# DRAM scratch in blocks of 512 elements, and the prompt's values read back from the output

## The chip, the core and the metric

The kernel runs on one core of a Trainium2 chip. A core has five engines with a queue of instructions each: TensorE (PE in the profile, with its weight loads as PEld), VectorE (DVE), ScalarE (ACT), GpSimd (POOL) and SyncE (SP). DMAs are issued from SyncE's queue nearly always, some from ScalarE's, and run on 16 DMA engines. The metric is device time in microseconds, lower is better.

## What is computed

One step of a decoder with two layers over a prompt of 2048 tokens and over 8 samples of 8 new tokens each, whose past of 4096 tokens lies in a paged cache. All data are 32-bit floats.

```python
# layer A: a gated linear recurrence; layer B: attention with forget gates
x = x + rms_norm(recurrent_mixer(rms_norm(x, a_pre_norm), ...), a_post_norm)
z = rms_norm(x, kv_norm) @ w_kv                  # the shared K, V and forget logits
k, v, logf = z[..., :1024], z[..., 1024:2048], log_sigmoid(z[..., 2048:] + b_f)
c = cumsum(logf)                                 # over the past and the new tokens
q, g = split(rms_norm(x, b_pre_norm) @ b_w_in)
s = q @ k.T * 64 ** -0.5 + c[query] - c[key]     # 16 heads of 64, causal
o = softmax(s) @ v
x = x + rms_norm((o * silu(g)) @ b_w_out, b_post_norm)
```

`k`, `v` and `logf` of the prompt and of the samples are outputs too. For the samples, keys and values of the past are gathered page by page (128 tokens a page) through a page table.

## The kernel before

The prompt passes in chunks through layer A (two of 1024 tokens) and through the projections of layer B (1024, 512 and 512 tokens, `phase_b`, L859). [...]

In `phase_b`, `token_major` (L885) makes `k` and `v` in tiles of 128 tokens by 256 columns: products into PSUM, a copy into the tile `kf` on ScalarE (L897), and a store of `kf` to the output tensor (L904). For keys, four such tiles are transposed on TensorE in `keys` (L871), split into a high and a low part (a sum of two reduced-precision numbers), and stored to the scratch `kd` (L882, L883). For values, a second store of the same tile goes to the scratch `vd` (L915), which has the layout of the output, one row of 1024 per token. `logf` (L817) makes the running sums of the forget logs and stores them in three parts as `ncd` (L852).

The prompt's attention (`attention`, L1309) runs over 16 heads, 4 query blocks of 512 in each, and key tiles of 128. Per head, `load_keys` (L1368) and `load_head` (L1375) bring the head's keys (`kbt`: high part and the three forget parts; `ka`: high and low parts interleaved) and its values (`vvt`) from scratch into SBUF, one head ahead of use. Head 0's loads are issued from ScalarE's queue, all others from SyncE's.

The samples' attention (`decode`, L1024) goes in 16 turns, one for each sample and each half of the heads. In a turn, 32 pages of keys and 32 of values (the half of the heads, 256 KB a page) come in as `raw` (L1074). The softmax of a turn (`softmax`, L1167) ends in a change of layout through DRAM: the transposed probabilities `sy` are stored to the scratch `pd` in four stores (L1217) and read back by one load as `sx` (L1218), which the value products (L1237) need. The scratch is doubled, so that turns alternate. The first two turns run beside the projections of the first chunk, the other 14 beside those of the second and third and beside the prompt's attention. `Side.along` (L1010) interleaves the two streams of instructions by estimated costs; the framework then orders each engine's instructions by a modelled timeline (L1828) and adds the semaphore waits. Issues on SyncE stay in that order, and one that waits holds all behind it.

At the end, `project` (L1599) multiplies the gated attention outputs with `b_w_out` and stores the result.

Of the kernel before, what the change touches and what calls it, by code (L numbers as in the profile page):

```python
# [20 lines left out]
P = 128  # L21
D = 1024
KB = 8
SEQ = 2048
# [3 lines left out]
H = 16  # L28
HD = 64
# [50 lines left out]
def f(ap):  # L80

    return ap.bitcast(F32)
# [3 lines left out]
def tile_hawk_fox(  # L86
# [8 lines left out]
    V, A, G, T, S = nc.vector, nc.scalar, nc.gpsimd, nc.tensor, nc.sync  # L95
# [9 lines left out]
    def tt(eng, out, a, b, op):  # L105
        eng.tensor_tensor(out, a, b, op=op)  # L106
# [18 lines left out]
    vp_flat = v_p.rearrange("o t h d -> (o t) (h d)")  # L125
# [28 lines left out]
    def dt_(name, shape):  # L154
        return dram.tile(shape, F32, name=name, tag=name)
# [6 lines left out]
    x1s_d = dt_("x1s", [NSAMP, D])  # L162
    x1_d = dt_("x1", [SEQ, D])

    kd_d, qd_d = dt_("kd", [D, 2, SEQ]), dt_("qd", [D, 2, SEQ])
    sg_d = dt_("sgd", [D, SEQ])
    v_d = dt_("vd", [SEQ, D])
    nc_d = dt_("ncd", [H, 3, SEQ])
    ks_d, vs_d = dt_("ksd", [NSAMP, D]), dt_("vsd", [NSAMP, D])

    qs_d = dt_("qsd", [DB, 32, 4, KB, DS])


    pd_d = [dt_(f"pd{i}", [4, 32, 4, 512]) for i in range(2)]

    c_d = dt_("cd", [2, 4, 4, DB, NPG // 4, 256])
    cn_d = dt_("cnd", [H, NSAMP])
# [40 lines left out]
    def tpp(name="tp"):  # L218
        return psum["mm"].tile([P, 512], F32, name=name, tag="tp", bufs=2)
# [597 lines left out]
    def logf(s, pool):  # L817

        z, mx, nt, sm = s.z, s.cols, len(s.tiles), s.samp
        e = pool.tile([P, nt, H], F32, name="ze", tag="ze")  # L820
        lf = pool.tile([P, nt, H], F32, name="lf", tag="lf")
        V.scalar_tensor_tensor(e[:], z[:], -1.0, z[:], op0=ALU.mult, op1=ALU.max)
        A.activation(e[:], e[:], AF.Exp, scale=-1.0)
        yield
        log1p_into(pool, lf[:], e[:], [P, nt, H])
        V.tensor_scalar(z[:], z[:], 1.0, 0.0, op0=ALU.mult, op1=ALU.min)
        tt(V, lf[:], z[:], lf[:], ALU.subtract)
        yield
        cf = pool.tile([H, mx], F32, name="cf", tag="cf")
        for i, (col, m, samp, tok) in enumerate(s.tiles):  # L830
            S.dma_start(lfs_flat if samp else lfp_flat[tok:tok + m], lf[:m, i, :])
        pts = [t for t in enumerate(s.tiles) if not t[1][2]]
        n4 = 0
        for g0 in range(0, len(pts), 4):
            grp = pts[g0:g0 + 4]
            ps = tpp("lt")
            for j, (i, (col, m, samp, tok)) in enumerate(grp):
                T.transpose(ps[:H, j * P:(j + 1) * P], lf[:, i, :], ident[:, :])
            w = len(grp) * P

            V.tensor_copy(cf[:, n4:n4 + w], ps[:H, :w])
            V.tensor_tensor_scan(cf[:, n4:n4 + w], cf[:, n4:n4 + w], cf[:, n4:n4 + w], ccar[:, 0:1],
                                 op0=ALU.add, op1=ALU.min)
            V.tensor_copy(ccar[:, 0:1], cf[:, n4 + w - 1:n4 + w])
            n4 += w
            yield

        V.tensor_scalar(cf[:, :n4], cf[:, :n4], -1.0, 0.0, op0=ALU.mult, op1=ALU.add)
        for j in range(3):
            c = pool.tile([H, mx], F32R, name="cpart", tag="cpart")  # L850
            V.tensor_copy(c[:, :n4], cf[:, :n4])
            S.dma_start(nc_d[:, j, s.t0:s.t0 + n4], f(c[:, :n4]))  # L852
            if j < 2:
                tt(V, cf[:, :n4], cf[:, :n4], f(c[:, :n4]), ALU.subtract)
            yield
        if sm:
            sample_c(pool, lf)

    def phase_b(s, x, feed, nk, early):  # L859
# [3 lines left out]
        with ExitStack() as es:  # L863
# [7 lines left out]
            def keys(grp, cc, fb):  # L871

                w = len(grp) * P
                ps = tpp("kt")
                for j, (kf, tok) in enumerate(grp):
                    T.transpose(ps[:, j * P:(j + 1) * P], kf[:, fb * P:(fb + 1) * P], ident[:, :])
                th = pool.tile([P, 512], F32R, name="kth", tag="fth", bufs=2)
                tl = pool.tile([P, 512], F32R, name="ktl", tag="ftl", bufs=2)
                evac_pair(th[:, :w], tl[:, :w], ps[:, :w])
                r0 = cc * 256 + fb * P  # L880
                tk = grp[0][1]
                S.dma_start(kd_d[r0:r0 + P, 1, tk:tk + w], f(th[:, :w]))  # L882
                S.dma_start(kd_d[r0:r0 + P, 0, tk:tk + w], f(tl[:, :w]))  # L883

            def token_major(kind, cc):  # L885

                nonlocal forget
                W = feed.take()
                isk = kind == "k"
                kfs = []  # L890
                w = WC if (kind, cc) == ("k", 0) else 256
                for i, (col, m, samp, tok) in enumerate(s.tiles):
                    ps = mmp("kv")
                    mm3(ps[:m, :w], lambda k: xh[:, k, col:col + m], lambda k: xl[:, k, col:col + m],
                        W.h(0, w), W.l(0, w), KB)
                    kf = pool.tile([P, 256], F32, name="kf", tag="kf", bufs=nk)
                    A.copy(kf[:m, :], ps[:m, :256])  # L897
                    if w > 256:
                        tt(V, s.z[:m, i, :], ps[:m, 256:w], bfB[:m, :], ALU.add)
                        if i == nt - 1 and not early:  # L900
                            forget = logf(s, pool)
                    sl = slice(cc * 256, (cc + 1) * 256)
                    dst = (ks_flat if samp else kp_flat[tok:tok + m]) if isk else (vs_flat if samp else vp_flat[tok:tok + m])
                    S.dma_start(dst[:, sl], kf[:m, :])  # L904
                    if samp:
                        S.dma_start((ks_d if isk else vs_d)[:, sl], kf[:m, :])
                        known.add((kind, cc))
                    elif isk:
                        kfs.append((kf, tok))
                        if len(kfs) == 4 or i == nt - 1:  # L910
                            for fb in range(2):
                                later.after(2 + fb, lambda grp=kfs, cc=cc, fb=fb: keys(grp, cc, fb))
                            kfs = []
                    else:
                        S.dma_start(v_d[tok:tok + m, sl], kf[:m, :])  # L915
                    later.tick()
                    if i == nt - 1 or i == 0:
                        feed.fetch()
                        feed.fetch()
                    if i >= 1:  # L920
                        feed.split()
                        feed.fetch()
                    next(forget, None)
                    yield 24 * 109
# [99 lines left out]
    def decode(es, turns, nraw, nktr, ahead):  # L1024
# [142 lines left out]
        def softmax(t):  # L1167
# [42 lines left out]
            sy = spare()[:, :].rearrange("p (a x h q) -> p a x h q", a=4, x=8, h=8)  # L1210
# [3 lines left out]
            sx = pool.tile([P, 4, 8, 8, DS], F32, name="sx", tag="sx")  # L1214
            pd = pd_d[(b * 2 + hg) % 2]
            for i in range(4):
                S.dma_start(pd[:, :, i].rearrange("a l f -> l a f"), sy[i * 32:(i + 1) * 32].rearrange("p a x h q -> p a (x h q)"))  # L1217
            S.dma_start(sx[:, :, :, :, :].rearrange("p i x h q -> p (i x h q)"), pd.rearrange("a l i f -> (a l) (i f)"))  # L1218
            pt = pool.tile([32, 8, 32], F32, name="dpt", tag="dpt")
            V.transpose(pt[:, :, :].rearrange("p h x -> p (h x)"), pn[:, :, :].rearrange("p h x -> p (h x)"))  # L1220
            pc = t.pc = pcs[(b * 2 + hg) % 2]
# [87 lines left out]
    def attention(es):  # L1309
# [10 lines left out]
        vvs = [pool.tile([P, 16, HD], F32, name=f"vvt{i}") for i in range(2)]  # L1320
# [5 lines left out]
        for i in range(NQ):  # L1326
            if i % 3 == 0 and i < 6:
                kb = kbs[i // 3]
# [37 lines left out]
        queue = [A]  # L1366

        def load_keys(h):  # L1368
            kb = kbs[h % 2]
            loaded.add(h)  # L1370
            for lo, hi in halves(h):
                queue[0].dma_start(f(kb[0:64, lo:hi]), kd_d[h * HD:(h + 1) * HD, 1, lo:hi])
                queue[0].dma_start(f(kb[64:67, lo:hi]), nc_d[h, :, lo:hi])

        def load_head(h):  # L1375
            hr = slice(h * HD, (h + 1) * HD)
            ka = pool.tile([P, SEQ], F32R, name="ka", tag="ka", bufs=2)
            for lo, hi in halves(h):
                queue[0].dma_start(f(ka[:, lo:hi]), kd_d[h * HD:(h + 1) * HD, :, lo:hi].rearrange("d x t -> (d x) t"))
            queue[0].dma_start(vvs[h % 2][:, :, :], v_d[:, hr].rearrange("(k p) d -> p k d", p=P))  # L1380
            heads[h] = ka

        def load_unit(u):
# [118 lines left out]
        def advance(tick):  # L1502
# [6 lines left out]
            while done[0] < min(need, len(tasks)):  # L1509
# [5 lines left out]
                done[0] += 1  # L1515

        load_keys(0)
        tick = 0
        advance(-1)
# [9 lines left out]
        for u, (h, qc) in enumerate(units):  # L1529
            load_low(u + 2)  # L1530
            for k in range(nks[u]):
                ka, kb = heads[h], kbs[h % 2]
                qa, qb = qas[u], qbs[u % NQ]
                lo = max(0, k - qc * 4) * P
# [7 lines left out]
                if k == 0:  # L1542
                    p = acc = pool.tile([P, 512], F32, name="acc", tag="acc", bufs=NACC)
                else:
                    p = pool.tile([P, 512], F32, name="p", tag="p", bufs=NP)
# [293 lines left out]
```

## Time and profile before

| | us |
|---|---|
| median of 3 runs | 3089.88 |
| lowest, highest | 3076.2, 3178.36 |
| the profiled execution | 3082.92 |
| its span, from the first to the last instruction | 3081.2 |
| mean granted TensorE clock in it | 0.965 of full speed |

The profile is of one execution. Its page has busy times per engine, the span in 40 slices (a digit is the busy share in tenths; the DMA row is the mean busy share of the 16 DMA engines), the DMA queues with their packets, and the chain of waits: the work that ended last, followed back from the last instruction to whatever released it at each step. In a group's row stand the line, the engine, the operation, what is written and read (`out<-in`), the count, busy time, the mean of one, and the idle time ahead of it with what ended it. Rows of DMA issues give the issuing time on the queue (SPq, ACTq) as least/median/greatest in ns, and the first and last start in us; the transfer itself runs later on the DMA engines.

### The profile page before, as it was taken

The numbers are of one execution on the slowest core, as the hardware profiler recorded it, in microseconds if no ns is written. First come the engines' busy times: TensorE is split into PE (matmuls) and PEld (weight loads), VectorE is DVE, ScalarE is ACT, GpSimd is POOL, SyncE is SP. The second block draws the span as 40 slices with busy tenths as digits, with TensorE's granted clock in tenths as the row PEclk, the third lists the DMA queues.
The fourth block names the chain that finished last, engine by engine and source line by source line (L and its number), as shares of the span: only waits on it lengthen the run. The fifth ranks groups of instructions, "written<-read, shape, count | busy, mean of one in ns | idle before, by whom it ended". The sixth has DMA issues, their size and how long they took to land.

```text
span 3081.2 us, 58151 instructions
## 1 busy us (share of the span) xinstructions
PE 2825.8 (92%) x20462; PEld 2177.5 (71%) x20462; DVE 1805.6 (59%) x4012; ACT 1295.0 (42%) x2874; POOL 1155.5 (38%) x1263
## 2 busy tenths in 40 slices
PE   6998999998999989997999799899999988999798
PEld 5997888988999978885797455455545554544587
DVE  7876555424367756755655666666667665543244
ACT  4665432232346655333333334444444445455211
POOL 1663101000025532000001456655656648788322
PEclk9999999999999999998999799999999999999899
DMA  4224547788622266999999998989999996331343
GB/s 121 89 76 150 154 137 216 242 267 254 198 84 86 79 195 198 327 305 315 325 331 307 292 303 261 289 268 321 289 294 314 317 295 211 97 87 41 96 135 111
DMA packets 492855, 653.25 MB, mean 212 GB/s; under 512 B 91100, under 2 KB 292829, under 8 KB 485286
## 3 DMA queue, kind: packets, MB, share of 16 engines
q1 hardware_dynamic: 488934, 643.87, 66.9%
q10 hardware_dynamic: 3340, 3.56, 0.4%
q8 instruction: 162, 2.65, 0.4%
q0 software_dynamic: 288, 2.10, 0.2%
q14 instruction: 131, 1.07, 0.1%
HBM read 513.82 MB, written 135.16 MB: 211 GB/s over the span
## 4 chain that ended last, share of the span: by engine, by line
PE 54%; DMA 20%; DVE 10%; ACT 5%; SPq 5%; issue 4%; POOL 2%; ACTq 0%; DVEq 0%; POOLq 0%
PE ops L1557 5%; DMA raw<-in_cache_k_dram 5%; PE y L368 4%; PE y L370 4%; PE y L369 4%; PE st L1537 3%; DMA raw<-in_cache_v_dram 3%; PE kv L369 3%; PE kv L368 3%; PE kv L370 3%; PE sx L1404 3%; PE dO L1237 2%; SPq L1074 2%; PE qg L368 2%; PE st L1538 2%
## 5 line engine op out<-in xcount | busy, mean ns | idle before, releaser
L106 POOL TENSOR_TENSOR acc<-acc,p 128x512 f32<-128x512 f32 (+3 forms) x576 | 638.8, 1109 | 291.7 <-PE ops L1557 226.4
L1546 ACT ACTIVATE p<-st 128x512 f32<-128x512 f32 (+3 forms) x576 | 290.4, 525 | 404.8 <-PE st L1538 188.6
L1159 DVE STREAM_TRANSPOSE ktr<-raw 128x1024 f32<-128x1024 f32 x256 | 305.4, 1223 | 161.3 <-DMA raw<-in_cache_k_dram 143.7
L1406 DVE TENSOR_REDUCE mxs<-sx 128x1 f32<-128x512 f32 x384 | 253.9, 680 | 143.5 <-PE sx L1404 142.5
L369 PE MATMUL kv<-wl,xh 128*128 128x256 f32 (+3 forms) x1088 | 309.1, 287 | 8.9 <-DVE wl L413 8.8
L368 PE MATMUL kv<-wh,xh 128*128 128x256 f32 (+3 forms) x1088 | 310.4, 290 | 5.7 <-ACT wh L412 5.3
L370 PE MATMUL kv<-wh,xl 128*128 128x256 f32 (+3 forms) x1088 | 309.2, 286 | 0.0
L1557 PE MATMUL ops<-p,vvt 128*64 128x512 f32 (+3 forms) x1152 | 292.7, 550 | 3.1 <-ACT p L1546 2.8
L1537 PE MATMUL st<-qa,ka 128*128 128x512 f32 (+3 forms) x640 | 273.3, 427 | 21.8 <-ACT p L1546 18.0
L1404 PE MATMUL sx<-kbt,qbt 96*128 96x512 f32 (+3 forms) x640 | 234.7, 426 | 26.1 <-DMA qbt<-qd 11.5
L1537 PEld LDWEIGHTS st<-qa,ka 128*128 128x128 f32 x640 | 123.6, 193 | 178.5 <-issue 112.1
L412 ACT ACTIVATE wh<-wst,gv 128x256 fp32r<-128x256 f32 (+1 forms) x384 | 164.4, 499 | 195.0 <-DMA wst<-in_b_w_in_dram 81.8
L1538 PE MATMUL st<-qbt,kbt 128*128 128x512 f32 (+3 forms) x640 | 237.0, 371 | 0.0
L413 DVE SCALAR_TENSOR_TENSOR wl<-wst,gv,wh 128x256 fp32r<-128x256 f32 (+1 forms) x384 | 169.9, 492 | 108.1 <-ACT wh L412 100.3
L368 PE MATMUL qg<-xh,wh 128*128 128x384 f32 (+2 forms) x640 | 229.1, 359 | 1.0 <-ACT wh L412 1.0
L370 PE MATMUL qg<-xh,wl 128*128 128x384 f32 (+2 forms) x640 | 227.5, 357 | 0.9 <-DVE wl L413 0.9
L369 PE MATMUL qg<-xl,wh 128*128 128x512 f32 (+2 forms) x640 | 226.9, 356 | 0.0
L1092 POOL TENSOR_TENSOR qw<-qb,amask 128x128 f32<-128x128 f32 x64 | 29.3, 465 | 498.8 <-PE dS L1127 258.0
L369 PEld LDWEIGHTS kv<-wl,xh 128*128 128x128 f32 (+1 forms) x1088 | 203.8, 188 | 12.7 <-DVE wl L413 10.4
L368 PEld LDWEIGHTS kv<-wh,xh 128*128 128x128 f32 (+1 forms) x1088 | 203.6, 189 | 11.8 <-ACT wh L412 6.0
L370 PEld LDWEIGHTS kv<-wh,xl 128*128 128x128 f32 (+1 forms) x1088 | 205.3, 189 | 3.9 <-issue 3.9
L1404 PEld LDWEIGHTS sx<-kbt,qbt 96*128 96x128 f32 x640 | 119.1, 203 | 94.4 <-DVE mxs L1406 25.1
(289 smaller groups left out, 6472.1 us busy)
## 6 DMA issues: line engine op xcount, KB each, us to landing
raw<-in_cache_k_dram SPq DMA_DIRECT2D x512, 256.0 KB
raw<-in_cache_v_dram SPq DMA_DIRECT2D x512, 256.0 KB
wst<-in_w_kv_dram SPq DMA_DIRECT2D x48, 512.0 KB
wst<-in_b_w_in_dram SPq DMA_DIRECT2D x48, 512.0 KB
xt<-in_x_prompt_dram SPq DMA_DIRECT2D x32, 512.0 KB
wst<-in_a_w_in_dram SPq DMA_DIRECT2D x64, 256.0 KB
x<-x SPq DMA_DIRECT2D x32, 512.0 KB
out_dram<-kf SPq DMA_DIRECT2D x128, 128.0 KB
```

Of the source, the lines that this page charges most:

```text
L106: eng.tensor_tensor(out, a, b, op=op)
L368: T.matmul(ps, lh(k), rh(k), start=(k == 0), stop=False)
L369: T.matmul(ps, lh(k), rl(k), start=False, stop=False)
L370: T.matmul(ps, ll(k), rh(k), start=False, stop=(k == nk - 1))
L413: V.scalar_tensor_tensor(wl[:, k, :], st[:, k, :], gk, f(wh[:, k, :]), op0=ALU.mult, op1=ALU.subtract)
L1159: V.transpose(t.kts[pp][:, n], raw[:, :, pp * 256:(pp + 1) * 256])
L1404: T.matmul(ps[:, :w], qb[0:96, j * P:(j + 1) * P], kb[0:96, ck * 512:ck * 512 + w], start=True, stop=True)
L1406: V.reduce_max(mx[:, j, ck:ck + 1], ps[:, :w], axis=AX.X)
L1537: T.matmul(ps[:, lo:], ka[:, ks], qa[:, lo:], start=True, stop=False)
L1538: T.matmul(ps[:, lo:], kb[:, ks], qb[:, lo:], start=False, stop=(k < qc * 4))
L1546: pair.append((k, lo, p, A.activation(p[:, lo:], ps[:, lo:], AF.Exp)))
L1557: return T.matmul(ops[r:r + HD, lo:], vvs[h % 2][:, k, :], p[:, lo:], start=(k < 2), stop=(last and k >= todo[-1][0] - 1))
```

## The change

The scratch tensors `kd` (keys) and `ncd` (forget parts) get an outer dimension of four blocks of 512 tokens; inside one block, rows of 512 elements follow each other. `pd` gets its dimension of four moved outermost, so that a row of 512 elements is contiguous and its neighbours are those of the same `i`. The tensor `vd` goes away with its store, and `load_head` reads the values from the output tensor. Stores and loads are rewritten for the new shapes. What a load brings, and where in SBUF it lands, stays as it was.

```diff
-    kd_d, qd_d = dt_("kd", [D, 2, SEQ]), dt_("qd", [D, 2, SEQ])
+
+    kd_d, qd_d = dt_("kd", [SEQ // 512, D, 2, 512]), dt_("qd", [D, 2, SEQ])
     sg_d = dt_("sgd", [D, SEQ])
-    v_d = dt_("vd", [SEQ, D])
-    nc_d = dt_("ncd", [H, 3, SEQ])
+    nc_d = dt_("ncd", [SEQ // 512, H, 3, 512])
...
-    pd_d = [dt_(f"pd{i}", [4, 32, 4, 512]) for i in range(2)]
+    pd_d = [dt_(f"pd{i}", [4, 4, 32, 512]) for i in range(2)]
...
-            S.dma_start(nc_d[:, j, s.t0:s.t0 + n4], f(c[:, :n4]))
+            S.dma_start(nc_d[s.t0 // 512:(s.t0 + n4) // 512, :, j].rearrange("c h t -> h c t"),
+                        f(c[:, :n4]).rearrange("h (c t) -> h c t", t=512))
...
-                S.dma_start(kd_d[r0:r0 + P, 1, tk:tk + w], f(th[:, :w]))
-                S.dma_start(kd_d[r0:r0 + P, 0, tk:tk + w], f(tl[:, :w]))
+                assert tk % 512 == 0 and w == 512
+                S.dma_start(kd_d[tk // 512, r0:r0 + P, 1], f(th[:, :w]))
+                S.dma_start(kd_d[tk // 512, r0:r0 + P, 0], f(tl[:, :w]))
...
-                    else:
-                        S.dma_start(v_d[tok:tok + m, sl], kf[:m, :])
...
-                S.dma_start(pd[:, :, i].rearrange("a l f -> l a f"), sy[i * 32:(i + 1) * 32].rearrange("p a x h q -> p a (x h q)"))
-            S.dma_start(sx[:, :, :, :, :].rearrange("p i x h q -> p (i x h q)"), pd.rearrange("a l i f -> (a l) (i f)"))
+                S.dma_start(pd[i].rearrange("a l f -> l a f"), sy[i * 32:(i + 1) * 32].rearrange("p a x h q -> p a (x h q)"))
+            S.dma_start(sx[:, :, :, :, :].rearrange("p i x h q -> p i (x h q)"), pd.rearrange("i a l f -> (a l) i f"))
...
-                queue[0].dma_start(f(kb[0:64, lo:hi]), kd_d[h * HD:(h + 1) * HD, 1, lo:hi])
-                queue[0].dma_start(f(kb[64:67, lo:hi]), nc_d[h, :, lo:hi])
+                cs = slice(lo // 512, hi // 512)
+                queue[0].dma_start(f(kb[0:64, lo:hi]).rearrange("d (c t) -> d c t", t=512),
+                                   kd_d[cs, h * HD:(h + 1) * HD, 1].rearrange("c d t -> d c t"))
+                queue[0].dma_start(f(kb[64:67, lo:hi]).rearrange("j (c t) -> j c t", t=512),
+                                   nc_d[cs, h].rearrange("c j t -> j c t"))
...
-                queue[0].dma_start(f(ka[:, lo:hi]), kd_d[h * HD:(h + 1) * HD, :, lo:hi].rearrange("d x t -> (d x) t"))
-            queue[0].dma_start(vvs[h % 2][:, :, :], v_d[:, hr].rearrange("(k p) d -> p k d", p=P))
+                queue[0].dma_start(f(ka[:, lo:hi]).rearrange("r (c t) -> r c t", t=512),
+                                   kd_d[lo // 512:hi // 512, h * HD:(h + 1) * HD].rearrange("c d x t -> (d x) c t"))
+            queue[0].dma_start(vvs[h % 2][:, :, :], vp_flat[:, hr].rearrange("(k p) d -> p k d", p=P))
```

## The prediction

> **What bounds the kernel now.** I read the page first, then stages of the span, then the chain of waits inside the stages in which transfers are heavy, then the instructions that the diff touches.
>
> ```profile
> span 3081.2 us, 58151 instructions
> ...
> PE 2825.8 (92%) x20462; PEld 2177.5 (71%) x20462; DVE 1805.6 (59%) x4012; ACT 1295.0 (42%) x2874; POOL 1155.5 (38%) x1263
> ...
> DMA  4224547788622266999999998989999996331343
> ...
> DMA packets 492855, 653.25 MB, mean 212 GB/s; under 512 B 91100, under 2 KB 292829, under 8 KB 485286
> ...
> q1 hardware_dynamic: 488934, 643.87, 66.9%
> ...
> PE 54%; DMA 20%; DVE 10%; ACT 5%; SPq 5%; issue 4%; POOL 2%; ACTq 0%; DVEq 0%; POOLq 0%
> ```
>
> TensorE is busy for 92% of the span, so only 255 us (3081.2 - 2825.8) of it can be recovered by moving work off its way. The DMA row says where: one stretch early (slices 8 and 9) and a long plateau of nines. Stages cut along that row show what each is short of (columns: stretch, length, busy us of PE, PEld, DVE, ACT, POOL with counts, granted clock, DMA share, GB/s).
>
> ```profile
> core 0: us, PE busy (x) PEld busy (x) DVE busy (x) ACT busy (x) POOL busy (x), PEclk, DMA share, GB/s
> 560.00:640.00 80.00, 80.00 (x890) 78.67 (x889) 31.97 (x63) 23.47 (x68) 1.71 (x5) 1.00 0.66 200
> 640.00:760.00 120.00, 109.42 (x1165) 102.49 (x1164) 45.64 (x80) 29.94 (x81) 0.00 (x0) 0.97 0.89 280
> 1240.00:1700.00 460.00, 430.07 (x3936) 368.47 (x3938) 271.06 (x524) 159.15 (x409) 20.09 (x35) 0.96 0.98 319
> 1700.00:2580.00 880.00, 793.91 (x6895) 452.28 (x6888) 584.74 (x1202) 375.81 (x912) 532.71 (x518) 0.94 0.94 293
> ```
>
> From 1240 to 2580 the DMA engines are busy 94 to 98% of the time. This is where the sample streams decode: pages of the cache pass beside the shared K/V and gate projections (to 1700) and beside the prompt's attention. TensorE is idle 29.9 us in the first part and 86.1 us in the second; in 640 to 760 it is idle 10.6 us, in 560 to 640 not at all. So two things are near their limit together, TensorE and the transfers. The chain of waits tells which of them ends last.
>
> ```profile
> by line: PE kv L368 17.6%; PE kv L369 17.4%; PE kv L370 17.3%; DMA out_dram<-kf 7.9%; PE dS L1127 5.5%; DMA raw<-in_cache_k_dram 5.1%; DMA raw<-in_cache_v_dram 4.5%; SPq L1074 3.4%; DMA sx<-pd 3.3%; DMA wst<-in_w_kv_dram 2.7%; issue 2.6%; D
> ...
> 637.78 10.92 DMA out_dram<-kf
> ...
> 749.10 5.06 DMA pd<-sy
> 754.23 6.51 DMA sx<-pd
> ```
>
> ```profile
> by line: DMA raw<-in_cache_k_dram 10.6%; PE ops L1557 7.4%; DMA raw<-in_cache_v_dram 6.4%; PE dO L1237 5.2%; SPq L1074 5.0%; PE st L1537 4.9%; DMA sc<-cd 4.6%; issue 4.4%; PE sx L1404 4.4%; PE dS L1127 4.3%; PE st L1538 3.3%; PE kv L369 2.5
> ...
> 1436.30 12.69 DMA sc<-cd
> ...
> 1858.83 10.82 DMA sc<-cd
> 2416.70 11.27 DMA kbt<-kd
> ```
>
> The first is 560 to 760, the second 1240 to 2580. In the second the pages, `sc` and SyncE's issues of pages alone hold 10.6 + 6.4 + 4.6 + 5.0 = 26.6% of the chain; in the first the store of `kf`, the pages, `sx` and those issues hold 24.2%. The chain changes hands between transfer and TensorE all the time, so a microsecond of DMA time taken out is worth more than a quarter and less than a whole one at the end.
>
> **The second copy of the values (L915).** The change removes 64 stores of 128 KB and their issues.
>
> ```profile
> L915 SPq DMA_DIRECT2D vd<-kf x64: 319/425/1352, 569.1 to 1649.9; - x64
> ```
>
> ```profile
> L915 SPq DMA_DIRECT2D vd<-kf x16: 422/424/1321, 569.1 to 627.9; - x16
> ```
>
> ```profile
> L915 SPq DMA_DIRECT2D vd<-kf x15: 326/440/1352, 703.7 to 757.6; - x15
> ```
>
> ```profile
> sx<-pd SPq DMA_DIRECT2D x16, 1024.0 KB
> ...
> ka<-kd SPq DMA_DIRECT2D x15, 1024.0 KB
> ...
> vd<-kf SPq DMA_DIRECT2D x64, 128.0 KB
> ...
> kbt<-kd SPq DMA_DIRECT2D x15, 512.0 KB
> ```
>
> Of the 64, 16 lie in 560 to 640, 15 in 640 to 760, one behind it, and the other 32 in the stage to 1700 (the last at 1649.9). The 16 are free: TensorE is busy 80.00 of 80.00 us there. The 15 are 15 x 0.131 MB = 1.97 MB, at that stage's 280 GB/s 7.0 us of transfer. The 32 are 4.19 MB, at 319 GB/s 13.1 us. Together 20.1 us of saturated DMA time. Their issues, 47 x 0.425 = 20.0 us of SyncE, run beside the transfers, so I don't add them. By the chain between a quarter (5 us) and all of the 20.1 us comes off the end. I take 14, nearer to all, because a DMA share of 0.98 is nearer to a transfer bound than TensorE's idle tells; the ceiling is TensorE's idle time in the two stages, 10.6 + 29.9 = 40.5 us.
>
> **Values read back from the output.** `load_head` (L1380) keeps its shape: rows of 4 KB pitch, pieces of one head. What is new is that it waits for the stores of L904 in place of those of L915.
>
> ```profile
> L904 SPq DMA_DIRECT2D out_dram<-kf x136: 332/377/1714, 409.5 to 1649.0; - x136
> ```
>
> ```profile
> L1380 SPq DMA_DIRECT2D vvt<-vd x15: 371/391/627, 1704.8 to 2760.7; - x15
> ```
>
> The last output store is issued at 1649.0, before the last store of the copy, and the first load comes 55 us after it: no wait. Behind a late one would stand the head's loads on ScalarE's queue (head 0) and the pages on SyncE's (the others); 55 us of cover against the longest landing on the chain, 12.69 us. Cost zero.
>
> **Keys, log-forget parts and P in blocks of 512.** The stores keep number and row size (2 KB rows of `kd`, four 256 KB stores of `pd`), only their pitch in DRAM falls. The loads change: a row of 8 KB becomes four rows of 2 KB.
>
> ```profile
> L1379 SPq DMA_DIRECT2D ka<-kd x12: 332/337/765, 1716.9 to 2574.3; - x12
> ```
>
> ```profile
> L1218 SPq DMA_DIRECT2D sx<-pd x14: 331/430/585, 1339.1 to 2539.4; - x14
> ```
>
> ```profile
> L1116 SPq DMA_DIRECT2D sc<-cd x14: 554/577/1557, 1260.5 to 2457.7; - x14
> ```
>
> In the plateau these are 12 heads x (1024 + 512) KB and 14 turns x 1024 KB: 33.6 MB, 4096 rows of 8 KB, 12,288 packets more. No row isolates the price of a 2 KB packet, so I bound it by what a busy DMA engine moves in stages of different mix, GB/s over 16 times the share. The plateau gives 293/(16 x 0.94) = 19.5 and 319/(16 x 0.98) = 20.3, mostly from pages; the lowest mix, with the 256-byte pieces of `vvt`, is
>
> ```profile
> 2580.00:2890.00 310.00, 280.77 (x1217) 147.59 (x1215) 140.26 (x325) 161.48 (x340) 245.68 (x215) 0.98 0.32 84
> ```
>
> 84/(16 x 0.32) = 16.4. For 2.10 MB on each engine that is 103, 108 and 128 us: from 4 us less to 20 us more than now. I take 0: a page of the cache arrives as rows of 8 x 64 x 4 bytes, 2 KB like the new ones, and the plateau's rate is mostly theirs. An issue with one more dimension could take as long as that of `sc`: 577 - 337 = 0.24 us on 12 x 2 + 14 issues, 9 us of SyncE, of which 5.0% (its share of the chain) is 0.5 us. `ncd` is three rows a head and counts for nothing.
>
> [...]
>
> **Sum.** -14 (copy) + 0 (read-back) + 0 (blocks) = -14 us. The profiled execution took 3082.92 us around its span of 3081.2; 3082.9 - 14 = 3069 us. The median of the runs shown is 3089.88, 7 us above that execution.
>
> **Rivals.** (1) Slower: blocks of one row come slower than a row in one piece. In the new `kd` the four pieces of a partition lie 1024 x 2 x 512 x 4 bytes = 4 MiB apart. For it: equal megabytes don't land equally fast here, `sx` in 6.51 us, `sc` (each block read eight times over) in 10.82 and 12.69, a factor of 1.7 to 1.9. Against it: the sixteen pieces that a partition of `vvt` gathers lie 512 KiB apart today, and the stage in which they weigh most is the one with 16.4. If the 33.6 MB took twice their time, at 293 GB/s that is 115 us; the plateau has no room for it, so it delays the pages behind. With 80% exposed (the DMA share is 0.94, TensorE covers some) +92 - 14 = +78, 3161 us. It passes 2% (62 us) when the loads take (62 + 14)/(115 x 0.8) = 83% longer.
>
> [...]
>
> (2) Faster by more than 2%: issue and transfer are in series, not side by side. Then 47 x (0.425 + 0.41) = 39 us goes with the copy. The rows
>
> ```profile
> PE dO L1237 <- DMA sx<-pd: 6.8, 1, 6.8
> ```
>
> ```profile
> SPq L1074 <- DMA sc<-cd: 32.2, 9, 4.4
> ```
>
> add to that: TensorE waits 6.8 us for `sx`, and a page's issue waits for transfers that it doesn't read (here `sc`, above the 10.92 us of the store of `kf`), as fewer DMAs would make rarer. 39 + 6.8 + half of 32.2 + 4 (the better end of the blocks) = 66: 3017 us. Against it: of those nine waits the change touches none directly.
>
> (3) Nothing moves: TensorE takes over wherever a store goes, 3083 us. And should the queue have cut 8 KB rows already, the blocks would do nothing; the count says it hasn't (492855 - 485286 = 7569 packets of 8 KB and more), so that has no chance of its own.
>
> **How the numbers follow.** Line 1828 has the program ordered by modelled durations, so removed stores and new shapes can also shift the order of issue by some waits like that of 10.92 us; two or three of them, 30 us either way, are what this adds. The forecast with (3) gets 0.57; its own range is 3042 (all 40.5 us of idle time) to 3103 (20 us for the blocks from 3083). Rival (2) gets 0.18 and (1) 0.25, more than its mechanism alone, since a shifted order that costs more than 62 us counts with it. Within 2% of 3089.88 (3028 to 3152), about what a measurement of this kernel can tell from no change, is thus 0.57. For 8 in 10 the range reaches down to 3010, past (2), and up to 3165, past (1).
>
> **What would show it.** Right: no `vd` row, 64 issues fewer on SyncE; TensorE's idle time in 1240 to 1700 smaller by some 10 us and in 640 to 760 by some 5; packets of 8 KB and more down to about 2,600, total about 645 MB; GB/s per busy engine in 1700 to 2580 still 19 to 20. Wrong by (1): that rate falls below 18 and `ka`, `kbt` and `sx` appear on the chain with 10 us and more. Wrong by (2): the plateau ends 50 us earlier. Wrong altogether: the pages' issues wait longer for unrelated transfers at places that the diff doesn't touch, which would be the order's doing.

## The result, and the profile after

| | before | changed | |
|---|---|---|---|
| median of 20 runs, us | 3082.52 | 3098.75 | |
| ratio of the changed kernel to before | 1 | 1.0056 | 95% interval 1.0043 to 1.0069 |
| profiled execution, us | 3082.92 | 3101.2 | |
| mean granted TensorE clock in it | 0.965 | 0.959 | |

The change made the kernel 17 us slower (0.0056 x 3080), where 14 us faster was forecast. The time lies inside the forecast's range, on the other side of no change. First the page of the changed kernel, the lines that answer to those of before.

```profile
span 3099.5 us, 58078 instructions
...
PE 2841.2 (92%) x20462; PEld 2183.3 (70%) x20462; DVE 1802.6 (58%) x4012; ACT 1293.2 (42%) x2874; POOL 1152.1 (37%) x1263
...
DMA  4225447687522266999999998899899986331243
...
DMA packets 498995, 644.86 MB, mean 208 GB/s; under 512 B 90075, under 2 KB 283612, under 8 KB 496399
```

The transfers changed as the diff says: 498995 - 496399 = 2596 packets of 8 KB and more are left, and 8.4 MB are gone. But look at TensorE: the same 20462 products take 2841.2 us and not 2825.8, 15.4 us more, while its idle time (span less busy) goes only from 255.4 to 258.3 us. Most of the 18 us that this execution lost is not waiting; the same products took longer.

The stages, cut as before (the columns are those of the prediction's table):

```profile
core 0: us, PE busy (x) PEld busy (x) DVE busy (x) ACT busy (x) POOL busy (x), PEclk, DMA share, GB/s
640.00:760.00 120.00, 111.80 (x1184) 104.78 (x1183) 45.97 (x80) 29.91 (x81) 0.00 (x0) 0.97 0.84 266
1240.00:1700.00 460.00, 427.54 (x3987) 367.44 (x3985) 277.10 (x532) 159.13 (x409) 28.18 (x48) 0.97 0.97 317
1700.00:2580.00 880.00, 792.05 (x6743) 447.50 (x6744) 569.35 (x1176) 365.46 (x893) 509.28 (x493) 0.92 0.93 289
```

A busy DMA engine moves 289/(16 x 0.93) = 19.4 GB/s in the last stretch (19.5 before). More products fit into 640 to 760 and 1240 to 1700 than before (1184 for 1165, 3987 for 3936), and fewer into the last (6743 for 6895), at a clock of 0.92 for 0.94. So something was gained early and more was lost late. The products that score the prompt's queries against its keys show how much. They are written to a PSUM tile that is also called `sx` (it is not the samples' `sx` that is read back from `pd`), from the start of the prompt's attention almost to its end. Their row in the kernel before, and then in the changed one (least/median/greatest ns of one product, then the start of the first and of the last in us):

```profile
L1404 PE MATMUL sx<-kbt,qbt x640: 218/398/796, 1713.5 to 2822.1; 96*128 96x512 f32 x128, 96*128 96x128 f32 x16, 96*128 96x384 f32 x16
```

```profile
L1408 PE MATMUL sx<-kbt,qbt x640: 218/398/797, 1702.3 to 2840.3; 96*128 96x512 f32 x128, 96*128 96x128 f32 x16, 96*128 96x384 f32 x16
```

The attention starts 11.2 us earlier and takes 1138.0 us where it took 1108.6: 29.4 us longer, and its last score product comes 18 us later.

### The profile page after: what moved, and what is told of

The parts are those of the page before. It is cut to its first block, busy times and chain, and to the rows that moved or that the text cites. A ratio compares the mean times of both kernels' runs of the same rounds, so it can differ in the third digit from the quotient of the medians.

```text
span 3099.5 us, 58078 instructions
## 1 busy us (share of the span) xinstructions
PE 2841.2 (92%) x20462; PEld 2183.3 (70%) x20462; DVE 1802.6 (58%) x4012; ACT 1293.2 (42%) x2874; POOL 1152.1 (37%) x1263
## 2 busy tenths in 40 slices
DMA packets 498995, 644.86 MB, mean 208 GB/s; under 512 B 90075, under 2 KB 283612, under 8 KB 496399
## 4 chain that ended last, share of the span: by engine, by line
PE 55%; DMA 20%; DVE 9%; ACT 6%; SPq 5%; issue 4%; POOL 2%; DVEq 0%; ACTq 0%; POOLq 0%
PE ops L1561 5%; DMA raw<-in_cache_v_dram 5%; DMA raw<-in_cache_k_dram 4%; PE y L368 4%; PE y L369 4%; PE y L370 4%; PE st L1541 3%; PE kv L368 3%; PE kv L369 3%; PE kv L370 3%; PE sx L1408 3%; PE dO L1237 3%; DMA sc<-cd 3%; PE dS L1127 2%; PE st L1542 2%
```

## The experiments

Ratios below are to the kernel before, run on the same chip (its medians there lay between 3078.9 and 3084.2 us), with 95% intervals.

### One part alone

`copy_only` leaves the copy out and reads the values from the output; `blocks_only` has only the new shapes of `kd`, `ncd` and `pd`.

```diff
-                        S.dma_start(v_d[tok:tok + m, sl], kf[:m, :])
+                        pass
...
-            queue[0].dma_start(vvs[h % 2][:, :, :], v_d[:, hr].rearrange("(k p) d -> p k d", p=P))
+            queue[0].dma_start(vvs[h % 2][:, :, :], vp_flat[:, hr].rearrange("(k p) d -> p k d", p=P))
```

> The second copy is gone and the values are read from the output; keys, forget parts and P keep their old layout. On every engine the planned order of instructions is that of the changed kernel. Theory O (order: taking the stores out makes the planner order the attention stage differently, and that order is worse there; the blocks cost nothing): slower than before by 0.3 to 0.8%, about as the change, with the projections done some 11 us earlier (last qg product at about 1682 us) and the last ops product some 15 us later. Theory B (blocks: rows of 2 KB instead of 8 KB cost some 29 us in the attention stage): 0.2 to 0.6% faster than before, since only the gain of 11 us is left.

> Keys, forget parts and P in blocks, the second copy kept and read. The planned order is exactly that of before on every engine. Theory O: the same time as before within 0.2%. Theory B: slower by 0.7 to 1.2%, all of it between the first and the last ops product.

`copy_only`: 1.0039 [1.0022, 1.0056]. `blocks_only`: 1.0019 [1.0003, 1.0035]. They add up to the change (1.0058 beside 1.0056), and the larger part of the loss comes from the part that I had booked as the gain. `readback_only` has the second of the two lines alone, `keys_blocks_only` the blocks of `kd` and `ncd` without `pd`:

> The second copy is still stored, but the values are read from the output. The planned order is exactly that of before. Theory O (order): the same time as before within 0.15%. Theory R (reading the output tensor is what costs in the run with the copy gone): slower by 0.3 to 0.9%, with the attention stage 20 to 30 us longer.

> Only the keys and the forget parts in blocks, P and the copy as before; the planned order is exactly that of before. If the 0.19% of blocks_only comes from the head's loads: 1.001 to 1.004. If it comes from P (sx, on whose arrival the value products wait): 1.000 within 0.001.

`readback_only`: 1.0000 [0.9982, 1.0018], so reading from the output costs nothing that can be seen (6 us would be). `keys_blocks_only`: 1.0017 [1.0001, 1.0033], as much as all blocks together. That points to the heads' loads and away from `pd`, but both intervals begin just above 1, and they don't show it.

### Is it the planned order?

With 64 stores fewer, the framework plans every engine's order anew. Listing the built programs side by side, `blocks_only` and `readback_only` have before's order on every engine to the last instruction; in `copy_only` 34% of TensorE's and 37% of SyncE's instructions stand elsewhere, and its order is that of the changed kernel. The first test turned the planning off in both kernels:

```diff
-    with _tile.TileContext(nc, schedule_with_timeline_sim=True) as tc:
+    with _tile.TileContext(nc, schedule_with_timeline_sim=False) as tc:
```

> The kernel before, ordered without the modelled timeline. No theory says how it stands to before (a different order over the whole program: 1 to 10% slower is likely); it is the reference for the next run.

> The changed kernel, ordered without the modelled timeline: apart from the 64 stores its order is nearly that of the previous run (2% of SyncE's and 5% of TensorE's rows moved). Theory O: 5 to 20 us faster than the previous run, since the stores' work is gone and the order stays. Theory B: 10 to 30 us slower than it.

Before 1.1064 [1.1047, 1.1082], changed 1.1008 [1.0988, 1.1028]. Without planning the two orders differ in 5% of TensorE's instructions, and there the changed kernel is 17 us faster than the one before. The second test made the planner draw other orders, by the constant that sets how much of the samples' work goes beside the prompt's, with and without the copy:

```diff
-SHARE = 1.13
+SHARE = 1.135
```

> The kernel before with a share of 1.135: every instruction and byte of before, in another order. Theory O: off before by 0.2 to 0.8%, either way. If order is worth nothing: within 0.15% of before.

> As the previous run, with a share of 1.135. The same expectations.

> The copy gone as in copy_only, and the share by which decode steps are interleaved with the prompt's work at 1.125 in place of 1.13: the same instructions and bytes as copy_only in another order. Theory O: the time moves with the order alone, to somewhere between 0.996 and 1.008 of before, at least 0.2% away from the 1.0039 of copy_only here or in the next run. Theory R, or any cost that comes with the instructions themselves: 1.004 within 0.0015, here and in the next run.

> The kernel before with a share of 1.125, the partner of copy_gone_share_lower (1.0010). Theory O (the copy's work is worth some 10 us, and what an order does to the attention stage is of the same size or more, either way): 0.996 to 1.012 of before, and over all pairs of equal share the kernel without the copy is the faster one more often than not. If leaving the copy out costs something of its own: 0.996 to 0.998, below its partner by the same 0.39% as at 1.13.

> The kernel before with a share of 1.10. As the previous run; its partner is the next.

> The copy gone, share 1.10. Theory O: within 1% of the previous run, more likely below it than above. If leaving the copy out costs something of its own: 0.2 to 0.6% above the previous run.

| `SHARE` | copy kept | copy gone |
|---|---|---|
| 1.10 | 1.0079 [1.0054, 1.0105] | 1.0105 [1.0075, 1.0135] |
| 1.125 | 0.9999 [0.9980, 1.0018] | 1.0010 [0.9989, 1.0031] |
| 1.13 | 1 | 1.0039 [1.0022, 1.0056] |
| 1.135 | 1.0117 [1.0092, 1.0142] | 1.0044 [1.0027, 1.0060] |

A step of 0.005 in a constant, with the same instructions, costs 1.2%. Taking the copy out goes either way. What an order costs can't be told in advance here: it is a draw, and that of before is among the best of these eight.

### Are SyncE's held queues the cause?

In the new order more pages stand ahead of most loads of `qa` and `ka` in the later heads, and these loads wait longer for TensorE to give their buffers back, with all later pages behind them. SyncE's waits between 1700 and 2620, before and then changed (us in total, times, longest):

```profile
SPq L1379 <- PE st L1540: 19.3, 5, 9.0
SPq L1392 <- PE st L1540: 15.6, 4, 8.3
```

```profile
SPq L1396 <- PE st L1544: 31.2, 6, 10.9
SPq L1382 <- PE st L1544: 25.5, 4, 17.3
```

34.9 us have become 56.7. Part of that is chance: in the trace of `readback_only`, which has before's order, they are 46.1 us. So I moved these loads to ScalarE's queue, where no page stands behind them:

```diff
-                queue[0].dma_start(f(qa[:, :]), qd_d[h * HD:(h + 1) * HD, :, qc * 512:(qc + 1) * 512].rearrange("d x t -> (d x) t"))
+                A.dma_start(f(qa[:, :]), qd_d[h * HD:(h + 1) * HD, :, qc * 512:(qc + 1) * 512].rearrange("d x t -> (d x) t"))
```

> The kernel before with the query loads of L1392 (tile qa) issued from ScalarE's queue instead of SyncE's. Theory W (what the order does is to hold SyncE: it stands at the loads of qa and ka until TensorE has let go of a buffer, 30 us in before and 47 to 50 us with the copy gone in waits over 4 us, and the pages queue behind): faster than before by 0.2 to 0.8%. Without W: as any other order, 0.998 to 1.012.

> The copy gone, and the loads of qa on ScalarE's queue. Theory W: 0.988 to 0.997 of before, and below the previous run, since the gain of the copy is no longer spent in SyncE's waits. Without W: 1.000 to 1.006, as the three orders of this kernel seen so far.

> As the previous run, with the key loads of L1379 (tile ka) on ScalarE's queue too. Theory W: as fast as the previous run or up to 0.3% faster (ka's waits are the other half). Without W: 1.000 to 1.006.

`qa` moved: 1.0149 [1.0129, 1.0169] with the copy and 1.0119 [1.0098, 1.0139] without; `ka` too: 1.0225 [1.0204, 1.0247]. Now the exponentials stand behind these waits. TensorE's waits for them in the attention stage (1700 to 2620), in the kernel before and then with `qa` moved:

```profile
PE ops L1557 <- ACT p L1546: 2.6, 6, 1.4
```

```profile
PE ops L1557 <- ACT p L1546: 35.8, 24, 6.4
```

33 us more of TensorE's waiting cover anything that the freed SyncE gained, and the planner drew a new order for these kernels too, so these runs say nothing for or against its waits as the cause. That stayed open.

### The order held fixed

The last three runs separate the two things that `copy_only` had changed together. The program is planned once, and then built again with the instructions of every engine tied to that order, one behind the other:

```diff
+    for k in order:
+        i = emitted[k]
+        j = last.get(i.engine)
+        if j is not None:
+            tc.add_manual_dep(i, j.name, mb.DependencyInfo(mb.DependencyClass.NoSync, mb.DependencyReason.DATA),
+                              reason="order")
+        last[i.engine] = i
```

Here `order` is the planned order of the other program. `copy_gone_old_order` is `copy_only` in before's order, `after_old_order` the whole change in before's order. `copy_kept_new_order` is the kernel before in the order of `copy_only`, each store of the copy right behind the output store of its tile.

> Second copy gone and values read from the output, with every engine's instructions held in the order that the kernel before has (the planned order of before is taken, the 64 stores are left out of it). Theory O (removing the stores gains what the prediction's sum gave, 14 us, and the new plan is what costs): 0.9955 (3065 us), between 0.993 and 0.998; granted clock 0.966 as before. Theory N (the stores were hidden and their removal gains nothing; what copy_only showed is then the whole price of the new plan, 12 us): 1.0000, within 0.002. Theory T (before's order fits only with its own stores in it; any removal disturbs it): 1.003 or more. Theory C (what a plan costs is paid through TensorE's clock, as waits of 2 us and more are followed by stretches at half clock): time at half clock in the trace within 15 us of before's 215 us, where copy_only has 239 us.

> The whole change (blocks, no second copy, read-back), with every engine's instructions held in the order of the kernel before. Theory O: 0.9955 plus the 0.0019 of the blocks = 0.9974 (3071 us), so the change as written would be a gain of 8 us without its new plan. Theory N: 1.002. Theory T: 1.005 or more, as in the changed kernel (1.0056). Theory C: time at half clock 215 to 230 us, where the changed kernel has 255 us.

> The converse: the second copy is kept and read, but every engine follows the order planned for the kernel without it, each store of the copy right behind the output store of the same tile. Theory O: the new plan's price without the gain, 0.0039 + 0.0045 = 1.0084 (3105 us), granted clock 0.960 to 0.963. Theory N: 1.0039, as copy_only. Theory T (an order fits the work it was planned for): above 1.010.

| | before's order | order planned without the copy |
|---|---|---|
| copy kept | 1 | 1.0085 [1.0066, 1.0104] |
| copy gone | 0.9958 [0.9942, 0.9975] | 1.0039 [1.0022, 1.0056] |
| copy gone, with blocks | 0.9986 [0.9973, 1.0000] | 1.0056 [1.0043, 1.0069] |

Down the columns, the copy's removal gains 0.0042 and 0.0046: 13 to 14 us in either order. Across, the order costs 0.0085, 0.0081 and 0.0070: 22 to 26 us. The blocks cost 0.0028 and 0.0017 here and 0.0019 with the copy kept: 5 to 9 us. From the top left to the bottom right the steps are -13 + 25 + 5 = 17 us. Such a sum comes out by construction; what shows that the parts are separate is that each costs the same wherever it is taken, within the intervals. The tie itself has no run of its own, but it can hardly cost anything: a price of its own would make the copy's gain smaller in the left column and larger in the right one, by twice that price between them if the gain is the same in both orders, and the two gains differ by 0.0004 (with some 0.003 either way). And 3071.54 us beside 3084.17 is the best kernel of this study: leave the copy out, keep the shapes and the order.

The rows of `sx` place it. In turn `copy_gone_old_order`, `copy_kept_new_order` and `copy_only`:

```profile
L1404 PE MATMUL sx<-kbt,qbt x640: 219/399/797, 1700.8 to 2807.9; 96*128 96x512 f32 x128, 96*128 96x128 f32 x16, 96*128 96x384 f32 x16
```

```profile
L1404 PE MATMUL sx<-kbt,qbt x640: 220/399/797, 1713.2 to 2845.4; 96*128 96x512 f32 x128, 96*128 96x128 f32 x16, 96*128 96x384 f32 x16
```

```profile
L1404 PE MATMUL sx<-kbt,qbt x640: 220/398/797, 1699.4 to 2827.0; 96*128 96x512 f32 x128, 96*128 96x128 f32 x16, 96*128 96x384 f32 x16
```

With the old shapes the attention starts at 1699 to 1701 where the copy is gone and at 1713 where it is kept, in either order. In before's order it then takes 1107.1 us (1108.6 in the kernel before), in the other order 1132.2 and 1127.6. Among these four the copy sets the start and the order the length of the stage.

Kernels in one order can also be compared product by product, the n-th of TensorE with the n-th. From the product that starts at 1240 us to the one at 1700, `copy_gone_old_order` gains 10.2 us on the kernel before, and `copy_only` gains 16.9 on `copy_kept_new_order`. From 640 to 760 they gain 3.3 and lose 2.4, which is no more than `readback_only`, with all of before's work, differs from before there (3.0). So the gain of the copy is seen in 1240 to 1700, and in 640 to 760 it isn't.

With the blocks the picture is less clean. The rows of `blocks_only` and of `after_old_order`, both in before's order:

```profile
L1410 PE MATMUL sx<-kbt,qbt x640: 220/397/797, 1703.0 to 2818.6; 96*128 96x512 f32 x128, 96*128 96x128 f32 x16, 96*128 96x384 f32 x16
```

```profile
L1410 PE MATMUL sx<-kbt,qbt x640: 220/398/796, 1690.4 to 2812.3; 96*128 96x512 f32 x128, 96*128 96x128 f32 x16, 96*128 96x384 f32 x16
```

Both start 10 us earlier than the same kernel without blocks (1713.5 and 1700.8), and both lose that again in a longer stage (1115.6 and 1121.9 us). In the new order the blocks bring no earlier start (1702.3 beside 1699.4). Each is one trace, and where the blocks gain and lose was not looked into.

### What the order's price is made of

First the pages of `copy_gone_old_order` and of `copy_kept_new_order`, the two ends:

```profile
span 3065.3 us, 58063 instructions
...
PE 2822.8 (92%) x20462; PEld 2177.6 (71%) x20462; DVE 1803.0 (59%) x4012; ACT 1294.9 (42%) x2874; POOL 1152.8 (38%) x1263
```

```profile
span 3104.7 us, 58159 instructions
...
PE 2837.7 (91%) x20462; PEld 2180.0 (70%) x20462; DVE 1800.7 (58%) x4012; ACT 1294.2 (42%) x2874; POOL 1154.9 (37%) x1263
```

TensorE idles 242.5 and 267.0 us, and works 2822.8 and 2837.7 us on the same products. About half of the second difference is the granted clock: the two traces stand 205 and 228 us at half speed, which by the figures below is 7 to 8 of the 15 us. The trace records it in stretches of 1.0 or 0.5 and nothing between, the shortest and most frequent at half speed 3.4 us (34 of the 72 at half speed in the traces of the kernel before and the changed one); a mean of 0.959 over 3099.5 us is thus 2 x 0.041 x 3099.5 = 254 us at half speed, and 216 us in the kernel before. One place in the changed kernel shows what brings it on. Stretches of its attention stage (columns as above):

```profile
2090.00:2102.00 12.00, 11.07 (x139) 6.44 (x137) 7.55 (x13) 2.23 (x5) 9.22 (x11) 1.00 0.94 320
2102.00:2112.00 10.00, 5.31 (x13) 3.10 (x12) 9.08 (x24) 4.95 (x20) 0.00 (x0) 0.55 0.99 182
2112.00:2122.00 10.00, 4.49 (x19) 2.76 (x23) 4.22 (x13) 2.74 (x7) 0.00 (x0) 0.50 0.82 253
2122.00:2132.00 10.00, 10.00 (x81) 5.58 (x76) 7.64 (x14) 4.80 (x11) 5.77 (x5) 0.93 1.03 329
```

and TensorE's timeline there (start, duration, what; idle time ahead of it and who ended it in brackets):

```profile
2106.17 0.59 PE L1183 MATMUL dm<-ident,dmr 128*128 128x8 f32 x2 [3.89 <-DVE dmr L1182]
...
2120.77 1.51 PE L1237 MATMUL dO<-raw,sx 128*32 128x256 f32 x12 [5.14 <-DMA raw<-in_cache_v_dram]
```

TensorE waits 3.89 us for the negated row maxima of a sample's softmax (`dmr`) on VectorE and 5.14 us for a page. With these two waits the clock stands at 0.5 for 20 us; of those 20 us TensorE works 9.8, on 32 products, and at half speed. So these waits cost their 9.03 us and then some of the work behind them. Over the 20 traces of this study, from 60 us on, 99% of the 293 TensorE gaps of 3 us and more that began at full clock were followed by a stretch at half clock (one that began in the gap or within 3.5 us behind it), 73% of the 263 gaps between 2 and 3 us, and 9 to 18% of those under 1 us; 88% of the 773 stretches at half clock have a gap of 1 us or more within 3.5 us ahead of them. TensorE's busy time follows the time at half clock through these 20 traces with 0.30 us for each us (0.36 without the two unplanned kernels).

By the mean clock of all runs (0.9656 before, 0.9607 in `copy_kept_new_order`) the new order puts TensorE at half speed for 244 us and not 212; at 0.30 to 0.36 that is 10 to 12 of the 26 us. The traces, one for each kernel, put 12, 18 and 14 us of the order's price on TensorE's busy time (2837.7 beside 2825.8, 2841.3 beside 2822.8, and 2841.2 beside 2827.0 in `after_old_order`), so some of the longer busy time isn't explained by the clock. The rest are the waits themselves. One kind stands out in every kernel of the new order: `sx` waits for VectorE to take the row maxima out of its three buffers. TensorE's waits in the attention stage, for the kernel before, `copy_gone_old_order`, `copy_only`, `copy_kept_new_order` and the changed kernel:

```profile
PE sx L1404 <- DVE mxs L1406: 6.5, 10, 1.3
```

```profile
PE sx L1404 <- DVE mxs L1406: 7.6, 9, 1.5
```

```profile
PE sx L1404 <- DVE mxs L1406: 12.1, 19, 2.2
```

```profile
PE sx L1404 <- DVE mxs L1406: 11.8, 18, 1.9
```

```profile
PE sx L1408 <- DVE mxs L1410: 12.7, 16, 3.7
```

Nine and ten waits in the old order, 16 to 19 in the new. In all six traces of the old order this row stands at 4.5 to 7.8 us (in 9 to 14 waits), in the three of the new at 11.8 to 12.7. That is about 5 us. That the plan has put scoring steps of the prompt where VectorE is still at the samples' work would explain it, and was not shown. SyncE's waits for `qa` and `ka` also part the orders, less cleanly: 34.9 us before and 47.4 in `copy_gone_old_order`, 56.7 to 58.5 in the three of the new order, and the 12.5 us between the first two cost nothing at the end. Which of the moved instructions make up what remains, up to some 10 us, wasn't found.

## Why the prediction was wrong

**The copy, -14 us: right.** Measured -13 and -14 us with the order held fixed (5 to 8 us either way), and it comes ahead of the attention, in the stage from 1240 to 1700 that held the larger part of the sum; of the smaller part, in 640 to 760, nothing could be seen. That 14 was hit so closely is in part luck, as it was a choice between 5 and 20. The mark that I named for it was poor: TensorE's idle time in 1240 to 1700 didn't fall by 10 us (460 - 427.5 = 32.5, before 29.9), as fixed stretches of a schedule that has moved hold other work. The start of a stage can be compared, a fixed stretch can't.

**The planner, 0: the step that failed.** The forecast knew that "removed stores and new shapes can also shift the order of issue" and charged it as a spread of "30 us either way" around nothing. It cost 22 to 26 us. The size was inside the spread; the error was the centre and the chance. The order of before is one of the best draws (best or equal best of the eight in the table, five of the others clearly slower), so a new draw is more often worse: the centre lay above zero, and the copy's 14 us don't outweigh what this draw cost. It was also charged as waits at their own length; the clock behind them was left out, and TensorE's busy time was taken as fixed, so that "only 255 us of it can be recovered" was no fixed bound: the busy time itself moved between 2822.8 and 2841.3 us. The mark that was named for the order's doing, longer waits of the pages' issues, didn't show it: from 1240 to 2620 the issues of L1074 waited 114.9 us before (85.7 for transfers) and 106.3 in the changed kernel (91.5 for transfers).

**The read-back, 0: right.** 1.0000 alone, with 0.0018 either way.

**The blocks, 0: too low.** 5 to 9 us, each with 5 to 7 us either way, inside the bounds of -4 to 20. Rival (1) didn't come: 19.4 GB/s per busy engine in 1700 to 2580, with the four pieces of a partition 4 MiB apart, and 19.5 before. The interval of `blocks_only` reaches from 1 to 11 us; what a packet of 2 KB costs by itself, no run shows.

**Rivals (2) and (3).** Issue and transfer were not in series: with the order fixed the gain is 13 us and not 39 or more. Nor did the gain vanish.

## What to carry to other kernels

Where a planner orders the instructions by modelled durations, compare the planned orders before costing an edit: one that changes the order is a new draw, and from an order that is already among the best, most draws are worse. Measure the edit with the order held fixed, and keep the old order if the edit gains in it; here that turned a loss of 0.56% into a gain of 0.42% for the one part that pays. And where TensorE is the bound, charge a wait of 2 us or more with the half-speed stretch that followed most of them here (73% of those of 2 to 3 us, 99% of the longer ones), and look at busy time as well as idle time: the same products took 2822.8 to 2841.3 us.

## What was unexpected of the hardware

Besides the clock, a queue that stands still behind one kind of load. On SyncE of the changed kernel, the issue behind a head's values (2048 pieces of 256 bytes):

```profile
1793.37 0.39 SPq L1384 DMA_DIRECT2D vvt<-out_dram  x1
1793.98 9.31 SPq L1390 DMA_DIRECT2D qbt<-qd  x1
```

The load itself is issued in 0.39 us; the next issue, which moves another tensor, then takes 9.31 us. It is so in the kernel before as well: behind 14 of its 15 loads of values the next issue takes over 2 us (up to 8.3), and behind no other tensor's DMAs is that the rule (at most 1 in 4, for `xh` and `xl`). So the change has no part in it. That the small pieces are the reason is a guess, and whether a head's values in longer pieces would free SyncE wasn't tried.
